# Two layers of a hybrid backbone: the state-space core begun group by group, with the second layer's z columns between the recurrence's

## The chip, the cores and the metric

The kernel runs on one core of one Trainium2 chip. The time is the device time of one execution in microseconds; a version is judged by the median of its runs. An execution's own time is a little longer than its span, which runs from the first to the last instruction in the profile.

## The reference

Two layers work on 256 context tokens and 256 latent tokens of 2048 channels, in float32. In each layer the tokens are normalised and modulated (scale and shift from a conditioning vector), and multiplied by `w_in`. The result's columns feed three groups of heads:

- a gated linear recurrence over time in both directions (columns `lx`, and `lg` for its gate);
- windowed attention with sinks, 8 heads over 2 key heads (`q`, `k`, `v`, and `ag` for its gate);
- a state-space model in both directions, two groups of 8 heads (`x`, `B`, `C`, `dt`, and `z` for its gate).

The state-space part, cut to what matters:

```python
xs, B, C = split(silu(conv(xbc)))            # x: 1024 channels, B and C: two groups of 128
dt = softplus(dt + bias)
for chunk in chunks of 128 tokens:           # forward and backward
    W = (C @ B.T) * decay * dt               # inside the chunk
    y = W @ x + (C @ h) * exp(Acs)           # h: the state that enters the chunk
    h = exp(A_last) * h + B.T @ (x * w_state)
y = rmsnorm(y * silu(z), norm_w)
```

Channels 512g to 512g + 511 of `x` belong to group g, with row block g of `B` and of `C`. The three results, gated, are multiplied by `w_out`, scaled by a gate from the conditioning vector and added to the tokens. The second layer gives latent tokens alone, so its `C`, `z`, `lg`, `q` and `ag` are computed for 256 tokens only, while `B`, `x`, `lx`, `k` and `v` need all 512.

## The kernel before

**Columns.** `w_in` is taken in columns of 128 channels. Each is 16 blocks (128 input channels each) and three matmuls a block (`mm3`): the float32 operands are split into a rounded part `hi` and a remainder `lo`, and hi x hi, hi x lo and lo x hi are summed in one PSUM accumulator (`acc`, three of them). Weights come in tiles `raw` of 8 blocks (512 KB, three buffers); ScalarE makes `hi` (line 237) and VectorE `lo` (line 238). A column is 512 tokens wide, or 256 where layer 2 needs the latent tokens alone. `HEAD` columns (B0, B1, C0, C1, x0, x1, and in layer 1 with `FILL` also x2 to x5) are built side by side over the input channels; `body` lists the others in order, the remaining x first, then lx and lg in pairs, z, k, v, then q and ag in pairs. After that comes the output projection in three parts, for the recurrence, the state-space part and the attention, 16 columns of 8 blocks each.

**Order of work.** TensorE's instructions stand in the order in which the program writes them (`manual_schedule`). What a finished column sets off is a generator (`consume` spawns it), which yields either a time in us or a condition. The planner's clock advances with each matmul by its nominal time (`mm`: 512 columns 0.216 us, four times that for plain float32, less where matmuls run side by side). After each block `pump` steps the tasks whose time has come, and the matmuls they write stand there in TensorE's order. The times are in `WAIT`, one for each layer. `drain(until)` steps the waiting tasks in order of their due times, moves the clock to each, and goes on until its condition holds; no column stands between. The other engines' instructions are ordered by the framework's scheduler, except those given to `keep_in_program_order`: such a one stays behind the instruction that was written before it for its engine.

**State-space core** (`ssd_core`, `State`, `Output`). It waits until 13 tasks have ended (two B, two C, eight x, dt), then goes through group 0 and group 1: 14 steps a group in layer 1, and 10 in layer 2, where the context's outputs aren't needed. A step has a `begin` (VectorE, ScalarE and GpSimd work; an `Output` also loads two tiles `bc` of running sums, broadcast to all partitions) and an `end` (matmuls). Between a step's `begin` and the next lies `WAIT["core"]`; a step's `end` follows one such wait after the next step's `begin`. When all steps have ended, `core_done` is set. `z` columns come behind a drain for `core_done`; `ssd_z` forms z * (1 + tanh(z / 2)) and multiplies `Y` by it. The square sums of `Y` are collected, and at z7 the norm follows.

**Conditioning products** (`ada_wide`). The modulation of layer 2 and both gates are products of a 256 KB row tile `araw` with a broadcast row `adac` on VectorE, summed along the row (line 380); these instructions are kept in program order. Parts 0 to 2 run in layer 1 from the core's end on. Part 3, layer 2's gate, is 64 products in four rows of 16, begun at the end of layer 2's head; after each comes `WAIT["ada1"]`, or `WAIT["ada"]` (5.97 in layer 2) once the core has ended, and it pauses from the core's beginning until its end:

```python
yield self.wait("ada" if self.core_done else "ada1")
if self.ssd_ready == 13 and not self.core_done:
    yield lambda: self.core_done
```

The output projection of layer 2 needs that gate to empty its first accumulator (line 1073), and begins so:

```python
self.drain(lambda: part in self.parts_done)
if pi == 0:
    self.drain(lambda: self.ada_done >= (4 if l else 1))
```

**Attention.** `att_q` writes a head's score matmuls, and then its softmax on VectorE, ScalarE (exp, line 854) and GpSimd (line 864). After `WAIT["q2"]` it writes the transposes (line 870), then the products with v. For head 7 the wait is `WAIT["q2z"]`, 12.98 in layer 2, so that these come after the first blocks of the output projection.

**Buffers.** `SHARED` gives tiles that don't live at the same time one set of buffers: `bc` (four) is shared with `dtw`, `adac`, `kh`; `aw` (three) holds `araw`, `ww` and `part0`; four PSUM tiles `mx` serve all matmuls but the columns'.

## Time and profile before

| | |
|---|---|
| median of 3 runs | 1846.21 us (1844.5 to 1850.26) |
| the profiled execution | 1850.27 us, span 1848.5 us |
| TensorE matmul busy | 1777.5 us, 96% of the span |
| VectorE busy | 1424.8 us, 77% |
| ScalarE busy | 959.7 us, 52% |
| GpSimd busy | 334.9 us, 18% |
| HBM read and written | 310.51 MB and 10.63 MB, 174 GB/s over the span |

Busy is the time in which an engine had an instruction in work; matmuls are pipelined and their ends are modelled, so a busy TensorE isn't TensorE at its best. The granted clock is the share of TensorE's full clock (2.4 GHz) that the throttle gave; the other level is 1.2 GHz, or 0.5. A chain is followed back from the last instruction to what released it. In a list of waits, a wait is put down to whatever came last.

### The profile page before, as it was taken

The numbers are of one execution on the slowest core, as the hardware profiler recorded it, in microseconds if no ns is written. First come the engines' busy times: TensorE is split into PE (matmuls) and PEld (weight loads), VectorE is DVE, ScalarE is ACT, GpSimd is POOL, SyncE is SP. The second block draws the span as 40 slices with busy tenths as digits, with TensorE's granted clock in tenths as the row PEclk, the third lists the DMA queues.
The fourth block names the chain that finished last, engine by engine and source line by source line (L and its number), as shares of the span: only waits on it lengthen the run. The fifth ranks groups of instructions, "written<-read, shape, count | busy, mean of one in ns | idle before, by whom it ended". The sixth has DMA issues, their size and how long they took to land.

```text
span 1848.5 us, 29534 instructions
## 1 busy us (share of the span) xinstructions
PE 1777.5 (96%) x10522; PEld 1456.0 (79%) x10522; DVE 1424.8 (77%) x3053; ACT 959.7 (52%) x1766; POOL 334.9 (18%) x271
## 2 busy tenths in 40 slices
PE   7999999999999999999999999999999999999999
PEld 4777876666778877887878887878666788999999
DVE  4447769899998888989999547776778885788765
ACT  4324577777433354555232335544687763677543
POOL 0000124434210022221000020010243330122000
PEclk9999999999999999999999999999999999999999
DMA  9982433435775645557777443464343564555656
GB/s 377 365 295 69 124 97 106 129 111 157 220 219 175 192 145 174 172 166 245 231 221 221 129 126 107 142 183 150 96 136 109 160 202 152 174 174 165 210 184 183
DMA packets 140261, 323.09 MB, mean 175 GB/s; under 512 B 14000, under 2 KB 39504, under 8 KB 139472
## 3 DMA queue, kind: packets, MB, share of 16 engines
q1 hardware_dynamic: 140112, 321.20, 55.6%
q8 instruction: 82, 1.34, 0.3%
q14 instruction: 67, 0.55, 0.1%
HBM read 310.51 MB, written 10.63 MB: 174 GB/s over the span
## 4 chain that ended last, share of the span: by engine, by line
PE 74%; DVE 12%; ACT 7%; issue 4%; DMA 3%; POOL 1%; SPq 0%; POOLq 0%; DVEq 0%; ACTq 0%
PE acc L174 57%; PE mx L174 12%; DVE lo L238 3%; PE ada L174 3%; PE mx L170 2%; DVE ee L1161 1%; DVE ada L380 1%; ACT lt L712 1%; DVE araw L380 1%; ACT hi L237 1%; DMA bc<-acsD 1%; ACT ww L1163 1%; DMA araw<-in_adaw_dram 1%; DVE lh L730 1%; ACT ee L1160 1%
## 5 line engine op out<-in xcount | busy, mean ns | idle before, releaser
L174 PE MATMUL acc<-u,hi 128*128 128x512 f32 (+1 forms) x4800 | 1284.7, 356 | 10.7 <-ACT hi L237 6.2
L174 PEld LDWEIGHTS acc<-u,hi 128*128 128x128 f32 x4800 | 840.6, 191 | 158.3 <-issue 29.0
L174 PE MATMUL acc<-u,lo 128*128 128x512 f32 (+1 forms) x2400 | 848.8, 354 | 24.8 <-DVE lo L238 24.2
L237 ACT ACTIVATE hi<-raw 128x512 fp32r<-128x512 f32 x640 | 399.3, 629 | 588.4 <-PE acc L174 459.2
L238 DVE TENSOR_TENSOR lo<-raw,hi 128x512 fp32r<-128x512 f32 x640 | 470.1, 737 | 195.7 <-ACT hi L237 186.0
L174 PEld LDWEIGHTS acc<-u,lo 128*128 128x128 f32 x2400 | 458.0, 191 | 98.9 <-DVE lo L238 39.0
L380 DVE SCALAR_TENSOR_TENSOR araw<-araw,adac 128x512 f32<-128x512 f32 x256 | 189.5, 741 | 8.6 <-DMA araw<-in_adaw_dram 5.3
L380 DVE SCALAR_TENSOR_TENSOR ada<-araw,adac 128x512 f32<-128x512 f32 x192 | 143.1, 745 | 11.2 <-DMA araw<-in_adaw_dram 6.6
L174 PE MATMUL mx<-u,hi 128*128 128x512 f32 (+1 forms) x320 | 98.8, 392 | 0.0
L1073 DVE SCALAR_TENSOR_TENSOR X<-acc,mod,X 128x256 f32<-128x256 f32 x144 | 65.0, 478 | 38.2 <-PE acc L174 38.0
L864 POOL TENSOR_SCALAR prob<-prob,qrs 128x512 f32<-128x512 f32 (+1 forms) x48 | 58.3, 1228 | 200.0 <-ACT hi L237 158.0
L427 POOL TENSOR_TENSOR ssq<-ssq,sq 128x512 f32<-128x512 f32 (+1 forms) x26 | 32.7, 1257 | 303.2 <-ACT sq L423 303.2
L1172 POOL TENSOR_TENSOR bc<-bc,CT 128x512 f32<-128x512 f32 x40 | 62.2, 1566 | 88.2 <-ACT bc L1171 49.1
L511 POOL TENSOR_SCALAR X<-xs,prm 128x512 f32<-128x512 f32 (+1 forms) x16 | 15.4, 963 | 344.5 <-DVE xs L489 340.6
L174 PEld LDWEIGHTS mx<-u,hi 128*128 128x128 f32 x320 | 55.9, 188 | 14.1 <-issue 4.0
L720 POOL TENSOR_TENSOR la<-lt 128x512 f32<-128x512 f32 x32 | 39.0, 1221 | 134.5 <-ACT lt L718 117.1
L174 PE MATMUL mx<-u,lo 128*128 128x512 f32 (+1 forms) x160 | 60.7, 379 | 0.0
L1161 DVE SCALAR_TENSOR_TENSOR ee<-bc,nacs,ee 128x128 f32<-128x128 f32 x96 | 44.2, 509 | 18.7 <-DMA bc<-acsD 14.3
L767 POOL TENSOR_TENSOR qw<-qw,cst 128x256 f32<-128x256 f32 x20 | 22.5, 1127 | 195.2 <-DVE rt L766 131.5
L727 POOL TENSOR_TENSOR lt<-lt,ltl 128x512 f32<-128x512 f32 x32 | 47.8, 1515 | 48.4 <-ACT ltl L724 45.5
L712 ACT ACTIVATE lt<-mx,gbh 128x512 f32<-128x512 f32 x64 | 42.4, 674 | 10.0 <-PE mx L174 10.0
L174 PE MATMUL mx<-xc,gw 64*64 64x512 f32 x128 | 39.9, 615 | 4.6 <-DVE H L1128 2.2
(236 smaller groups left out, 1979.0 us busy)
## 6 DMA issues: line engine op xcount, KB each, us to landing
raw<-in_w_in_dram SPq DMA_DIRECT2D x224, 512.0 KB, 3.7
araw<-in_adaw_dram SPq DMA_DIRECT2D x256, 256.0 KB, 3.2
raw<-in_w_out_dram SPq DMA_DIRECT2D x96, 512.0 KB, 3.8
ar<-in_ada_dram SPq DMA_DIRECT2D x84, 256.0 KB, 5.9
bc<-acsD SPq DMA_DIRECT2D x48, 256.0 KB, 4.1
ar<-in_ada_dram SPq DMA_DIRECT2D x22, 512.0 KB, 7.4
adac<-condD SPq DMA_DIRECT2D x28, 256.0 KB, 4.6
gw<-in_gates_dram SPq DMA_DIRECT2D x16, 256.0 KB, 2.9
```

The costliest lines, as they stand in the source:

```text
L170: self.nc.tensor.transpose(out=out, in_=lhsT, identity=rhs)
L174: self.nc.tensor.matmul(out=out, lhsT=lhsT, rhs=rhs, start=start, stop=stop, **kw)
L237: nc.scalar.activation(out=hi, in_=part, func=AF.Copy)
L238: nc.vector.tensor_tensor(out=lo, in0=part, in1=hi.bitcast(F32), op=ALU.subtract)
L380: i = nc.vector.scalar_tensor_tensor(out=o, in0=raw, scalar=1.0, in1=row[c].rearrange("p t x -> p (t x)"), op0=ALU.mult, op1=ALU.mult, acc ...
L712: nc.scalar.activation(out=t, in_=pg[g], func=AF.Tanh, scale=0.5, bias=self.gb[:, 16 * g + 8 * d + m:16 * g + 8 * d + m + 1])
L720: nc.gpsimd.tensor_tensor(out=a2, in0=tr, in1=tr, op=ALU.mult)
L727: nc.gpsimd.tensor_tensor(out=ti, in0=ti, in1=tl[:, d], op=ALU.mult)
L864: nc.gpsimd.tensor_scalar(out=pr[j], in0=pr[j], scalar1=rs[:, j:j + 1], scalar2=1.0, op0=ALU.mult, op1=ALU.mult)
L1073: nc.vector.scalar_tensor_tensor(out=x[:, s], in0=acc[:, s.start - w0:s.stop - w0], scalar=mod[:, 2 * KT + m, c:c + 1], in1=x[:, s], op0=A ...
L1161: nc.vector.scalar_tensor_tensor(out=e[:, j], in0=bcs[1][:, j], scalar=k.nacs[:, r:r + 1], in1=e[:, j], op0=ALU.add, op1=ALU.min)
L1172: nc.gpsimd.tensor_tensor(out=bc, in0=bc, in1=k.CT[:, g, None, tok].to_broadcast([P, 4, P]), op=ALU.mult)
```

## The change

`ssd_ready` was a count and is now a set of what has ended. The core waits, before each group, for that group's own B and C, for dt, and for its own four x columns. `core_begun` is set at the first group, and the conditioning products of layer 2 pause from then on. The wait between two core steps goes from 4 to 5.4 in layer 1, and from 5.2 to 9.2 in layer 2. In layer 2 each z column follows its lx and lg in `body`; z * (1 + tanh(z / 2)) is written to the context half of `Y`, which is idle in layer 2, and `Y` is multiplied once the core has ended. The drain for `core_done` stands ahead of the first z column in layer 1 as before, and ahead of the first k column in layer 2.

```diff
--- before.py
+++ after.py
@@ -73,8 +73,9 @@
     done = HEAD[l] + FILL[l]
     b = [("x", i) for i in range(8) if ("x", i) not in done]
     for m in range(8):
-        b += [("lx", m), ("lg", m)]
-    b += [("z", i) for i in range(8)]
+        b += [("lx", m), ("lg", m)] + [("z", m)] * l
+    if l == 0:
+        b += [("z", i) for i in range(8)]
     b += [("k", 0), ("k", 1), ("v", 0), ("v", 1)]
     for m in range(8):
         b += [("q", m), ("ag", m)]
@@ -131,7 +132,7 @@
 
 HB = 3
 WAIT = {"B": (36.48, 14.89), "C": (28.19, 0.27), "x": (33.09, 10.71), "dt": (16.92, 0.59), "softplus":
-        (19.41, 30.37), "acs": (0.94, 0.68), "core": (4, 5.2), "ada": (2.38, 5.97), "ada1": (1.17, 2.75), "z":
+        (19.41, 30.37), "acs": (0.94, 0.68), "core": (5.4, 9.2), "ada": (2.38, 5.97), "ada1": (1.17, 2.75), "z":
         (4.45, 7.93), "lx": (12.81, 15.41), "lx2": (1.16, 0.85), "k0": (6.3, 7.38), "k1": (1.19, 1.72), "k2": (1.86,
         2.04), "k3": (0.82, 6.16), "v": (7.89, 1.43), "q0": (2.04, 1.29), "q1": (5.86, 3.7), "q2": (7.82, 11.04),
         "q2z": (42.1, 12.98), "q3": (0.5, 1.1), "q4": (2.82, 1.03)}
@@ -382,7 +383,7 @@
                                                            op1=ALU.mult, accum_out=sums[:, c, m, q:q + 1])
                         self.tc.keep_in_program_order(i)
                     yield self.wait("ada" if self.core_done else "ada1")
-                    if self.ssd_ready == 13 and not self.core_done:
+                    if self.core_begun and not self.core_done:
                         yield lambda: self.core_done
             mod = self.mods[l][:, KT * part:KT * part + KT]
             o = PARAMS["ada_b"][0] + KT * part
@@ -512,7 +513,7 @@
                                     op0=ALU.mult, op1=ALU.mult)
             yield self.wait("x")
             self.tok_major(xs, self.Xtok[:, :, i * P:(i + 1) * P])
-        self.ssd_ready += 1
+        self.ssd_ready.add((kind, i))
 
     def dt_weights(self, l):
         nc = self.nc
@@ -586,7 +587,7 @@
         self.acsD = self.dram([P, P], "acsD")
         nc.sync.dma_start(out=self.acsD, in_=at)
         yield self.wait("acs")
-        self.ssd_ready += 1
+        self.ssd_ready.add(("dt", 0))
 
     def softplus(self, z, n, tag):
 
@@ -612,9 +613,11 @@
     def ssd_core(self, l):
 
 
-        yield lambda: self.ssd_ready == 13
         ends = []
         for g in range(2):
+            need = {("B", g), ("C", g), ("dt", 0)} | {("x", 4 * g + i) for i in range(4)}
+            yield lambda: need <= self.ssd_ready
+            self.core_begun = True
             f1, r1 = self.ssd_state(0, g, 0), self.ssd_state(1, g, 1)
             steps = [f1, r1]
             if l == 0:
@@ -645,7 +648,7 @@
     def ssd_z(self, l, i, pz, t0):
         nc = self.nc
         th = self.t([P, 512], "cth")[:, t0:]
-        zz = self.t([P, 512], "cv")[:, t0:]
+        zz = self.Y[:, i, :C] if l else self.t([P, 512], "cv")
         nc.scalar.activation(out=th, in_=pz, func=AF.Tanh, scale=0.5)
         nc.vector.scalar_tensor_tensor(out=zz, in0=th, scalar=1.0, in1=pz, op0=ALU.add, op1=ALU.mult)
         if not self.core_done:
@@ -947,8 +950,8 @@
         nc = self.nc
         self.l = l
         mod = self.mods[l]
-        self.ssd_ready = self.kv_ready = 0
-        self.core_done = False
+        self.ssd_ready, self.kv_ready = set(), 0
+        self.core_begun = self.core_done = False
         self.lru_h, self.att_o, self.parts_done, self.mixes = {}, {}, set(), {}
         t0 = lambda kind: 0 if l == 0 or kind in CTX_COLS else C
         wst = self.blocks(self.a["w_in"][l], NW)
@@ -1035,7 +1038,7 @@
             self.spawn(self.ada_wide((0, 1, 2)))
         for ct in body(l):
             s = t0(ct[0])
-            if ct == ("z", 0):
+            if ct == (("z", 0), ("k", 0))[l]:
                 self.drain(lambda: self.core_done)
             if ct == ("k", 0):
                 self.att_begin(l)
```

## Rows read from the trace of the kernel before

**Rows 1.** The page, part 4: the chain that ended last, by engine.

```profile
PE 74%; DVE 12%; ACT 7%; issue 4%; DMA 3%; POOL 1%; SPq 0%; POOLq 0%; DVEq 0%; ACTq 0%
```

**Rows 2.** Stages: length; PE, PEld, DVE, ACT, POOL busy; clock; DMA share; GB/s.

```profile
218.00:474.00 256.00, 238.83 (x1255) 172.31 (x1252) 219.30 (x395) 184.39 (x356) 97.38 (x69) 0.99 0.43 130
...
1219.00:1271.00 52.00, 49.51 (x217) 39.83 (x216) 36.70 (x71) 21.98 (x43) 9.35 (x8) 0.93 0.59 181
1271.00:1475.00 204.00, 191.36 (x1139) 146.72 (x1138) 159.61 (x264) 147.74 (x255) 67.85 (x54) 0.97 0.41 125
1475.00:1530.00 55.00, 50.08 (x384) 46.57 (x383) 44.68 (x74) 35.18 (x62) 16.00 (x15) 0.97 0.66 203
1530.00:1704.00 174.00, 173.07 (x1235) 161.92 (x1234) 129.06 (x289) 110.76 (x211) 37.45 (x34) 1.00 0.54 164
```

**Rows 3.** Readers of finished columns, layer 2: count, ns min/median/max, first and last start.

```profile
L460 ACT ACTIVATE cv<-acc,scwh x6: 759/762/772, 1208.2 to 1271.9; 128x512 f32<-128x512 f32 x6
...
L649 ACT ACTIVATE cth<-acc x8: 367/370/385, 1481.0 to 1529.4; 128x256 f32<-128x256 f32 x8
...
L895 ACT ACTIVATE agt<-acc x8: 384/385/386, 1592.2 to 1704.5; 128x256 f32<-128x256 f32 x8
```

**Rows 4.** Waits of TensorE, 1219 to 1530: us in total, times, longest.

```profile
PE acc L174 <- DVE lo L238: 9.3, 10, 2.3
...
PE mx L174 <- ACT lt L712: 3.9, 4, 1.4
```

**Rows 5.** VectorE by line, 1284 to 1460: count, busy us, mean ns, idle before.

```profile
L238 DVE TENSOR_TENSOR lo<-raw,hi 128x512 fp32r<-128x512 f32 x56 | 47.8, 857 | 11.6 <-ACT hi L237 9.5 <-PE acc L174 2.0
...
L1164 DVE SCALAR_TENSOR_TENSOR ww<-cbm,dt,ww 128x128 f32<-128x128 f32 x32 | 10.1, 364 | 0.6 <-ACT ww L1163 0.6
...
L1147 DVE TENSOR_TENSOR cbm<-mx,cst 128x128 f32<-128x128 f32 x8 | 1.9, 277 | 0.0
```

**Rows 6.** Line 380 in 1160 to 1231, to 1290, and 1450 to 1704.

```profile
L380 DVE SCALAR_TENSOR_TENSOR araw<-araw,adac x19: 674/684/883, 1163.8 to 1226.2; 128x512 f32<-128x512 f32 x19
...
L380 DVE SCALAR_TENSOR_TENSOR araw<-araw,adac x32: 674/684/1787, 1163.8 to 1275.9; 128x512 f32<-128x512 f32 x32
...
L380 DVE SCALAR_TENSOR_TENSOR araw<-araw,adac x32: 672/684/1782, 1460.2 to 1677.3; 128x512 f32<-128x512 f32 x32
```

**Rows 7.** Timeline of TensorE, ScalarE and GpSimd, 1698 to 1714: start, length, instruction.

```profile
1699.88 0.40 PE L174 MATMUL mx<-kh,ql 128*128 128x512 f32 x1
...
1705.38 0.40 PE L174 MATMUL acc<-u,hi 128*128 128x256 f32 x2
...
1708.13 0.77 ACT L854 ACTIVATE prob<-mx,qng,qsc 128x512 f32<-128x512 f32 x1
...
1710.94 2.56 POOL L864 TENSOR_SCALAR prob<-prob,qrs 128x512 f32<-128x512 f32 x2 [13.87 <-DVE qrs L858]
```

**Rows 8.** The page, part 6: DMA issues, KB each, us from issue to landing.

```profile
araw<-in_adaw_dram SPq DMA_DIRECT2D x256, 256.0 KB, 3.2
...
bc<-acsD SPq DMA_DIRECT2D x48, 256.0 KB, 4.1
```

**Rows 9.** The chain in order of time, its last long piece: start, us, what.

```profile
1722.67 122.06 PE acc L174 x1017
```

**Rows 10.** Busy time in two short stretches, columns as in rows 2.

```profile
1243.00:1247.00 4.00, 1.70 (x6) 0.99 (x7) 3.63 (x6) 4.00 (x8) 1.80 (x2) 0.85 0.11 20
1247.00:1252.00 5.00, 5.00 (x14) 4.04 (x13) 4.93 (x8) 1.35 (x3) 2.53 (x2) 0.50 0.81 242
```

**Rows 11.** Timeline of SyncE's queue and VectorE, three rows of layer 2.

```profile
1276.60 0.33 SPq L1154 DMA_DIRECT2D bc<-acsD  x1
...
1434.36 0.90 SPq L1154 DMA_DIRECT2D bc<-acsD  x2
...
1448.79 0.68 DVE L1167 TENSOR_TENSOR ee<-ee,ww 128x512 f32<-128x512 f32 x1
```

**Rows 12.** Weight splits on VectorE over the whole span, columns as in rows 5.

```profile
L238 DVE TENSOR_TENSOR lo<-raw,hi 128x512 fp32r<-128x512 f32 x640 | 470.1, 737 | 195.7 <-ACT hi L237 186.0 <-PE mx L174 3.6 <-PE acc L174 2.0
```

## The prediction

> **What bounds the kernel now.** The page comes first, and on it the chain that ended last: 74% of the span is TensorE, 12% VectorE [rows 1]. Matmul work is unchanged by this diff, so only time in which TensorE stands still or runs at its lower clock can be won, and only time of the same two kinds can be lost.
>
> The table of stages says where such time is [rows 2]. In each stretch I take its length less PE's busy time, and add (1 - granted clock) x length. Layer 1, 218 to 474 us (x7 read to the last lg): 17.2 + 2.6 = 19.8 us. Layer 2, 1219 to 1271 (x4 to x7): 2.5 + 3.6; 1271 to 1475 (the lx/lg pairs, beside which the state-space core runs): 12.6 + 6.1; 1475 to 1530 (z): 4.9 + 1.6; together 31.5 us of 311. From 1530 to 1704 (k, v, q, ag): 0.9 us of 174. These are the ceilings of the gain: 31.5 and 19.8. The places of the stretches come from the instructions that read a finished column [rows 3]; the x columns stand 12.7 us apart, so x3, second of those six, is read near 1220.
>
> The list of PE's waits in 1219 to 1530 names VectorE's `lo` split as the largest (9.3 us in 10 waits) and further down the recurrence gates' tanh on ScalarE (3.9) [rows 4]: weights arrive late because VectorE is behind. Its queue in the core's stretch holds 56 splits at 857 ns, and eight lines of the core, from 10.1 us down to 1.9, 51 us in all [rows 5]. VectorE's busy time over the time PE needs (length less what was lost) is 159.6 / 185.3 = 86% in the core's stretch, and PE loses 9% there; it is 129.1 / 173.1 = 75% in 1530 to 1704, where PE loses 0.5% [rows 2].
>
> **What the change does, part by part.** *Core spread in layer 2.* It used to begin after x7; now it begins when B0, C0, dt and x0 to x3 are there, four columns earlier. By the planner's arithmetic (a column of 512 adds 48 x 0.216 = 10.4, of 256 5.2) x3's end to z7's end is 248 on the planner's clock: 4 x 10.4 for x4 to x7, 8 x 20.8 for the triples, 40 for gates, core and transposes. Twenty-one core intervals were 5.2 + about 1.4 each (their own matmuls 1.05, rounding to the next look at the tasks 0.35); now 9.2 + 1.4 = 10.6, 223 in all. Begun 12 after x3, the core ends at 235: 13 before z7 ends, so the drain moved to k0 finds nothing left. VectorE's work in 1219 to 1530 is 36.7 + 159.6 + 44.7 = 241 us, less some 23 ada products of 0.68 [rows 6] that move away, 225; PE needs 279.5: 81%, where the core's stretch had 86%. Between the two points above (0.5% lost at 75%, 9% at 86%), 81% gives 5%, some 13 to 14 us lost instead of 31.5. **Gain 18**; bounds 0 and 31.5.
>
> *Kept silu.* Eight 256-wide products go to the idle context half of `Y` instead of `cv`: same count, same size, nothing. When the core ends, seven pending `y` products of 256 columns come at once, about 0.4 us each as an estimate from 0.68 for 512 [rows 6]; columns already supplied hide them, and it is 3 us if that cover is gone.
>
> *Core spread in layer 1.* Begin moves from x7 + 33.1 to x3 + 33.1 on the planner's clock, about 25 earlier. Tasks are looked at every 0.647 in full columns, so 4 rounds up to 4.53 and 5.4 to 5.82, plus 1.0 of own matmuls: 29 intervals take 199 instead of 161, and the core ends about 13 later, 3 before z0's drain. No work moves between engines. VectorE stands at 219.3 / 236.2 = 93% there [rows 2], and falls to about 88% with x6 and x7's time taken in. That is no quiet stage either: **gain 6**, bounds 0 and 19.8. The ada products that wait for this core start 13 later and are all asked for only in the last columns of the layer's projection: nothing, 13 if that cover is gone.
>
> *What becomes late: the ada products of layer 2.* There are 64, pinned in VectorE's order, paused while the core runs. Before: 32 by 1276, before the core, and 32 from 1460 to 1677, 7.0 us apart (217.1 / 31), done 27 us before the last ag column is read [rows 3, 6]. After: the pause begins near 1231, where the trace has 19 [rows 6]. So 45 remain when the core ends, 13 us before z7's end. To the last ag column there are then 174 + 13 = 187 us, room for 27. **Eighteen are left** when `layer` reaches `drain(lambda: self.ada_done >= 4)`. This drain served nothing before.
>
> It serves tasks by due time and sets the clock to it: 18 steps of 5.97 move it by 107. Head 7 of the attention waits there too, due after 12.98 (q2z). So its transposes and products enter PE's order ahead of the output projection; before, 13 planner-us of the projection stood between. In the trace its last score matmul is issued at 1699.88, its exp runs at 1708.13, GpSimd's two scalings end at 1713.5, while PE had gone on at 1705.38 with the projection [rows 7]. Unsheltered, PE transposes at 1712.2 and, after copies, splits and the products, is free near 1716: 1716 - 1705.4, less 2.2 of head 7's own PE work, is 8.4; if ScalarE reaches the exp sooner, 4. Then some 15 ada products, behind head 7's gating in VectorE's order. A row takes 3.2 us to land [rows 8] and 0.68 to multiply; with three buffers and some 0.3 from product to next issue that is 1.4 each, the first three already there: 18 us, so the gate is ready near 1734. The projection's columns take 122.06 / 1017 x 24 = 2.9 us [rows 9] and three accumulators hold until 1716 + 8.7; then PE waits 9. Bounded by VectorE alone (15 x 0.68) it waits 2; behind weight loads, 16. Each of the two stalls can be followed by slow clock: after 2.3 us of idling in 1243 to 1247 the next 5 us were granted 0.50, the level of 1.2 GHz [rows 10], 3.4 us lost with its edges; I take 1 each, bounds 0 and 3.4. **Loss 19** (8.4 + 9 + 2), bounds 6 and 31.
>
> A rule that bears on this: the Trainium skill, "TensorE: Matmul & The Clock Gate", section "Part 2: What happens when you issue a matmul", says that only weight loads are pulled ahead while the matmuls themselves stay in program order. By it head 7's wait holds up the whole projection, as I count it; were matmuls free to pass, the first 8.4 would be nothing and the sum 8 lower. The waits on ACT `lt` in [rows 4], with ready columns behind them, agree with the rule.
>
> *A buffer held.* The old pause fell on a boundary of 16 products, where no `adac` row is live; 19 falls inside one, and `adac` shares four buffers with the core's `bc`. So the core of layer 2 has three, and the second half-group of each pair of outputs loads its last `bc` only when the first is finished, one step earlier. The trace shows such a buffer: the fourth `bc` load goes out at 1276.60, right behind the 32nd product [rows 6, 11]. From load to finished weights took 1434.36 to 1449.47, 15 us [rows 11]; at its shortest it is 4.1 to land [rows 8] and, as an estimate, 5 of arithmetic. A step is about 11.8 us in real time. Four such places: **loss 3**, bounds 0 and 14.
>
> *The sum.* -18 - 6 + 19 + 3 = -2 us against the profiled execution of 1850.3 us (span 1848.5 and 1.8 around it): 1848.3. The median of the three runs is 4.1 lower than that execution, so 1844.
>
> **The rivals.** *A, forecast, 0.40:* gains and the late drain nearly cancel; 1836 to 1852.
>
> *B, 0.20: the late products are mostly hidden.* ScalarE gives the exp early and rows land fast, so the drain costs 8: 1833. For it: DMA share is 0.54 there. Against: PE's order is fixed by the program.
>
> *C, 0.18, slower: the spread buys little.* Every VectorE product stays, and splits stay long: 857 ns in the core's stretch, with GpSimd's work beside them, against 737 over the whole kernel [rows 5, 12], which layer 1 at 93% does not escape. Layer 2 gains 8 and layer 1 2, so the drain decides: +12, 1858. It decides from where both gains are under 16. The Trainium skill, "SBUF — State Buffer", section "Who interferes with whom", gives such a mechanism: a VectorE instruction with two SBUF inputs and a GpSimd one that reads SBUF exclude each other. By it the spread moves these clashes and removes none, which would give C's 1858; 857 against 737 fits it.
>
> *D, 0.12, slower: three `bc` buffers bind.* At 15 us per chain, each of four places waits 3 us and idling drops the clock: +14 instead of +3, 1855. It decides from 2 us a place.
>
> *F, 0.10: the spread takes nearly all of it*, 28 and 14: -20, 1826.
>
> Against no change, 0.3% (5.5 us) is about what a measurement here can tell. Faster: 0.3 of A, 0.9 of B, all of F, 0.40. Slower: 0.2 of A, 0.9 of C, 0.75 of D, 0.33. Same: 0.27. The range leaves out half of F below and the far ends of C and D above: 1827 to 1861.
>
> **What would show it.** Right: PE's idle and half-clock time in the stage x4 to z7 falls below 20 us; 19 products of L380 before the core and some 18 after the last ag column; a PE gap behind head 7's `prob` and one behind `mod` in the first projection columns. Wrong: no such gaps (B), PE waits on `bc` or `ee` at every second output of layer 2 (D), or waits on `lo` unchanged (C).

## The result, and the profile after

The changed kernel takes 1887.79 us (median of 4 runs, 1885.62 to 1892.19), against 1846.27 for the kernel before on the same chip: a ratio of 1.0222, 95% interval 1.02 to 1.0244. That is slower, by 41 us, where 1844 was forecast, and outside the range. The profiled executions are 1885.62 and 1850.27 us, 35 apart.

Where do the 35 us lie? The readers of finished columns tell. Layer 2's first one stands 12 us later than before (1185.3, where it was 1173.3); its last z column 4 later, its last ag column 7 later; the first emptied accumulator of the output projection 39 later, and from the sixth on the distance stays at 35. The first three rows below are the columns x2 to x7 (with one of 256, a C column, ahead of them), z and ag as in [rows 3]; the last one, the accumulators, has its first start at 1747.3, where it was 1708.

```profile
L461 ACT ACTIVATE cv<-acc,scwh x7: 550/763/772, 1192.6 to 1283.3; 128x512 f32<-128x512 f32 x6, 128x256 f32<-128x256 f32 x1
L652 ACT ACTIVATE cth<-acc x8: 359/366/384, 1309.2 to 1533.1; 128x256 f32<-128x256 f32 x8
L898 ACT ACTIVATE agt<-acc x8: 384/385/388, 1599.7 to 1711.8; 128x256 f32<-128x256 f32 x8
L1076 DVE SCALAR_TENSOR_TENSOR X<-acc,mod,X x6: 475/484/484, 1747.3 to 1759.1; 128x256 f32<-128x256 f32 x6
```

The table of stages, cut at such readers (columns as in [rows 2]), first of the kernel before: layer 1 up to z0, layer 2 from x4 to z7, z7 to the last ag.

```profile
184.00:488.00 304.00, 286.83 (x1486) 210.03 (x1485) 259.37 (x474) 213.80 (x403) 106.23 (x78) 0.99 0.43 130
...
1232.00:1529.00 297.00, 276.95 (x1665) 221.80 (x1664) 231.24 (x388) 198.95 (x348) 90.45 (x74) 0.97 0.47 144
1529.00:1705.00 176.00, 175.07 (x1247) 163.70 (x1247) 130.98 (x294) 112.54 (x215) 37.45 (x34) 1.00 0.53 163
```

The same of the changed kernel, with a fourth row for the stretch up to the projection's first emptied accumulator:

```profile
184.00:502.00 318.00, 293.45 (x1480) 215.18 (x1480) 253.66 (x449) 213.30 (x402) 102.33 (x78) 0.95 0.37 118
...
1244.00:1533.00 289.00, 269.36 (x1650) 217.19 (x1649) 211.48 (x344) 191.35 (x336) 81.62 (x68) 0.98 0.41 128
1533.00:1712.00 179.00, 175.15 (x1242) 161.22 (x1241) 136.90 (x299) 118.48 (x223) 43.73 (x40) 1.00 0.55 175
1712.00:1747.00 35.00, 16.56 (x100) 15.37 (x98) 22.18 (x65) 10.41 (x25) 1.37 (x2) 0.65 0.64 211
```

Each stage's lost time is read from these rows: length less PE's busy time, plus half of the busy time at the lower clock (summed from the trace's clock records, since the clock's column is rounded). Layer 1: 18.9 before, 37.1 after. Layer 2, x4 to z7: 29.5 and 24.2. From z7 to the last ag: 0.9 and 3.8. Behind it: nothing, and 23.2 up to 1747, with 3.6 more up to 1880. The two parts move differently. Idle time alone goes from 17.2 to 24.6 in layer 1, and from 20.0 to 19.6 from x4 to z7; the clock's part goes from 1.7 to 12.5, and from 9.5 to 4.6. Stages called "x7 to z0" below start at 184; up to 217 no kernel here idles.

So layer 1 lost where a gain was forecast, layer 2 gained far less and won back no idle time to speak of, and the end cost more. The chain that ended last doesn't show where (76% PE where it was 74% [rows 1]); the list of PE's waits and its timeline name the end. First the waits of TensorE from 1700 to 1750, then its timeline:

```profile
PE acc L175 <- DVE X L1076: 11.7, 1, 11.7
PE mx L171 <- POOL prob L867: 6.6, 1, 6.6
```

```profile
1712.82 0.41 PE L175 MATMUL mx<-ptlh,vl 128*128 128x256 f32 x1
1719.80 1.97 PE L171 MATMUL mx<-cst,prob 128*128 128x128 f32 x8 [6.57 <-POOL prob L867]
...
1735.90 0.28 PE L175 MATMUL acc<-u,lo 128*128 128x256 f32 x1
1747.92 0.77 PE L175 MATMUL acc<-u,hi 128*128 128x256 f32 x2 [11.75 <-DVE X L1076]
```

Head 7's transposes hold PE until GpSimd has scaled its weights, with the projection's blocks behind them; then three full accumulators wait for the gate. VectorE's timeline shows what the gate waited for: late products, each behind its row's landing, then the sum.

```profile
1744.55 0.69 DVE L381 SCALAR_TENSOR_TENSOR araw<-araw,adac 128x512 f32<-128x512 f32 x1 [2.11 <-DMA araw<-in_adaw_dram]
...
1746.83 0.22 DVE L391 TENSOR_REDUCE mod<-adas 128x16 f32<-128x64 f32 x1
1747.08 0.17 DVE L392 TENSOR_TENSOR mod<-mod,prm 128x16 f32<-128x16 f32 x1
1747.29 1.27 DVE L1076 SCALAR_TENSOR_TENSOR X<-acc,mod,X 128x256 f32<-128x256 f32 x3
```

The count of products, against [rows 6]: 19 ahead of the core, 27 from its end to 1707, and 17 from 1715 on (the remaining one starts at 1711.5).

```profile
L381 DVE SCALAR_TENSOR_TENSOR araw<-araw,adac x19: 681/684/884, 1175.2 to 1244.1; 128x512 f32<-128x512 f32 x19
...
L381 DVE SCALAR_TENSOR_TENSOR araw<-araw,adac x27: 659/684/1230, 1516.4 to 1706.7; 128x512 f32<-128x512 f32 x27
...
L381 DVE SCALAR_TENSOR_TENSOR araw<-araw,adac x17: 682/692/694, 1715.4 to 1746.1; 128x512 f32<-128x512 f32 x17
```

### The profile page after: what moved, and what is told of

The parts are those of the page before. It is cut to its first block, busy times and chain, and to the rows that moved or that the text cites. A ratio compares the mean times of both kernels' runs of the same rounds, so it can differ in the third digit from the quotient of the medians.

```text
span 1883.6 us, 29522 instructions
## 1 busy us (share of the span) xinstructions
PE 1785.8 (95%) x10522; PEld 1462.2 (78%) x10522; DVE 1423.1 (76%) x3053; ACT 960.0 (51%) x1764; POOL 327.3 (17%) x271
## 4 chain that ended last, share of the span: by engine, by line
PE 76%; DVE 12%; ACT 4%; issue 4%; DMA 3%; POOL 1%; SPq 0%; DVEq 0%; POOLq 0%; ACTq 0%
PE acc L175 58%; PE mx L175 14%; DVE lo L239 3%; PE ada L175 2%; DMA araw<-in_adaw_dram 2%; PE mx L171 2%; DMA bc<-acsD 1%; DVE araw L381 1%; DVE ada L381 1%; DVE lh L733 1%; POOL prob L867 1%; DVE ee L1164 1%; DVE ww L1167 1%; DVE xc L467 1%; ACT hi L238 0%
## 5 line engine op out<-in xcount | busy, mean ns | idle before, releaser
L239 DVE TENSOR_TENSOR lo<-raw,hi 128x512 fp32r<-128x512 f32 x640 | 475.1, 746 | 204.3 <-ACT hi L238 191.3
L381 DVE SCALAR_TENSOR_TENSOR araw<-araw,adac 128x512 f32<-128x512 f32 x256 | 183.4, 718 | 14.1 <-DMA araw<-in_adaw_dram 8.6
L1076 DVE SCALAR_TENSOR_TENSOR X<-acc,mod,X 128x256 f32<-128x256 f32 x144 | 65.0, 478 | 36.7 <-PE acc L175 36.6
L1175 POOL TENSOR_TENSOR bc<-bc,CT 128x512 f32<-128x512 f32 x40 | 57.5, 1444 | 124.3 <-ACT bc L1174 95.3
L1164 DVE SCALAR_TENSOR_TENSOR ee<-bc,nacs,ee 128x128 f32<-128x128 f32 x96 | 37.9, 446 | 25.5 <-DMA bc<-acsD 22.2
L725 DVE SCALAR_TENSOR_TENSOR lt<-lt,xc 128x512 f32<-128x512 f32 x32 | 23.4, 731 | 27.8 <-ACT lt L715 27.8
```

The costliest lines, as they stand in the source:

```text
L239: nc.vector.tensor_tensor(out=lo, in0=part, in1=hi.bitcast(F32), op=ALU.subtract)
L381: i = nc.vector.scalar_tensor_tensor(out=o, in0=raw, scalar=1.0, in1=row[c].rearrange("p t x -> p (t x)"), op0=ALU.mult, op1=ALU.mult, acc ...
L1076: nc.vector.scalar_tensor_tensor(out=x[:, s], in0=acc[:, s.start - w0:s.stop - w0], scalar=mod[:, 2 * KT + m, c:c + 1], in1=x[:, s], op0=A ...
L1164: nc.vector.scalar_tensor_tensor(out=e[:, j], in0=bcs[1][:, j], scalar=k.nacs[:, r:r + 1], in1=e[:, j], op0=ALU.add, op1=ALU.min)
L1175: nc.gpsimd.tensor_tensor(out=bc, in0=bc, in1=k.CT[:, g, None, tok].to_broadcast([P, 4, P]), op=ALU.mult)
```

## The experiments

Ratios are to the kernel before, on the same chip, with their 95% intervals. The changed kernel has 1.0222. A string, below, is the eight ScalarE and nine VectorE instructions with which one `Output` forms its weights `ww` and `ee`. Lost times (us), as above:

| | ratio | layer 2 begins | x7 to z0 | x4 to z7 | z7 to ag |
|---|---|---|---|---|---|
| before | 1 | 0 | 18.9 | 29.5 | 0.9 |
| changed | 1.0222 (1.0200 to 1.0244) | +12 | 37.1 | 24.2 | 3.8 |
| layer 1 as before | 1.0140 (1.0123 to 1.0157) | +3 | 22.6 | 24.7 | 4.3 |
| layer 1: early begin alone | 1.0189 (1.0174 to 1.0204) | +5 | 28.4 | 28.7 | 4.6 |
| layer 1: wide steps alone | 1.0199 (1.0163 to 1.0234) | +10 | 40.9 | 23.9 | 4.5 |
| gate in time | 1.0100 (1.0076 to 1.0123) | +13 | 33.5 | 25.2 | 5.5 |
| gate in time, layer 1 as before | 1.0037 (1.0024 to 1.0050) | +3 | 20.4 | 22.8 | 5.0 |

The last four columns come from one execution each. Those with layer 1 untouched scatter from 18.9 to 22.6 in it, so 4 us there say little; their idle time alone is 15.9 to 17.2, the rest of the scatter is the clock's. From x4 to z7 the ten executions with the changed order and begin and with steps of 9.2 (these six, and four below) lose 22.8 to 28.7: 19.6 to 23.1 idle, and 1.5 to 8.1 through the clock.

**Layer 1.** Three kernels complete a table of two by two with the changed one.

```diff
-        "core": (5.4, 9.2)
+        "core": (4, 9.2)                 # first and second kernel
             need = {("B", g), ("C", g), ("dt", 0)} | {("x", 4 * g + i) for i in range(4)}
+            if l == 0:                   # first and third: all 13
+                need = {(k, i) for k in "BC" for i in range(2)} | {("dt", 0)} | {("x", i) for i in range(8)}
```

> The changed kernel with layer 1's core as it was: it begins when all 13 tasks have ended, and its steps are 4 apart; layer 2 stays changed. Theory (layer 1's core lost 12 us, from its x columns to layer 2's begin): those 12 come back whole, layer 2's first readers stand within 2 us of the kernel before, and the whole is 12 us under the changed kernel, 1874. Rival (layer 1's lag is a shift of transfers or of the modulation's products that only moves a wait from one layer to the other): the lag at layer 2's begin goes, but less than 6 us of it is left at the end, 1880 or more.

1875.9 us, and layer 2 begins 3 us late where the theory allowed 2: nearly as it said. The ratio falls by 0.8%, so the loss arises in layer 1 and isn't given back.

> The changed kernel with layer 1's steps 4 apart again, but begun group by group. Theory (the wider spacing costs: more columns have an Output's strings on VectorE and ScalarE beside them, so more of their splits come late): the loss goes, 1874, and the half clock in 217 to 492 us falls from 30 us of the time to under 10. Rival (the early begin costs: the core's work falls on the convolutions of x6 and x7 and on the transposes behind them): the loss stays, 1884 to 1888, and half clock stays above 20 us.

1884.1 us, the rival's time, but layer 2 begins 5 us late, not 12: neither holds. The early begin by itself costs something, though less than both edits; the next kernel tries the other one.

> The changed kernel, layer 1's core begun when all 13 tasks have ended, but its steps still 5.4 apart; with the changed kernel, the early begin alone and layer 1 as before it completes a table of two by two. Layer 2's first x columns were 12, 5 and 3 us later than before in those three. Theory (the two edits add up: the early begin some 4 us, the spacing some 5 to 7): 8 us later than before at layer 2's begin, 1880 us in all, and half clock in 217 to 492 us of some 15 us of the time. Rival (only both together hurt, since only then does the core lie beside the convolutions and reach into the last lx columns): 3 to 4 us later, 1875.

1886.1 us and 10 us late, beyond both: the spacing alone costs nearly all, so the two don't add up. Part of that is this kernel's own: its core isn't done at z0, and in the drain there PE waits for `ee`, 8.2 us in two waits (waits of TensorE, 184 to 507):

```profile
PE mx L175 <- DVE ee L1172: 8.2, 2, 7.0
```

**The end of layer 2.** Only the products' interval changes.

```diff
-        "ada": (2.38, 5.97)
+        "ada": (2.38, 3.0)
```

> The changed kernel with layer 2's conditioning products 3.0 apart behind the core in place of 5.97, so that all 64 are done before the last ag column and the last drain finds nothing to do. Theory (the end of layer 2 lost 28 us through that drain: head 7 ahead of the projection, the gate late, half clock behind each): all of it comes back, 1858, no gap behind prob or mod at the projection's begin. Rival (45 products in a shorter time fill VectorE beside the k, v, q and ag columns, where it stood at 136 of 178 us): PE loses 10 us or more from 1534 to 1712, and 1868 or more is left.

1866.5 us, 1.2% of 1846 or some 22 under the changed kernel; no gap behind `prob` or `mod` is left. The time lies between theory and rival, the mechanism is the theory's. From z7 to the last ag column 5.5 us are lost in place of 3.8. The drain is the cause of the end's loss; the denser products cost little.

> Both edits: layer 1 as before, and layer 2's conditioning products 3.0 apart behind the core. What is left of the change is layer 2's core begun early, its z columns between the recurrence's and the steps 9.2 apart. Theory (layer 2's part is worth 4 to 8 us once nothing else is lost): 1838 to 1842, under the kernel before. Rival (layer 2's part is worth nothing by itself, its 8 us at z7 are given back in k and v or come from VectorE's products moved behind): 1845 to 1850.

1856.6 us, ratio 1.0037: neither theory's time. With the same column matmuls from x4 to the last ag, this kernel needs 289 + 183 = 472 us and the kernel before 297 + 176 = 473. So layer 2's part, freed of the drain, is worth nothing: what is won ahead of z7 (half clock; the idle time is 21.1) is spent behind it.

> Layer 1 as before; in layer 2 the products are 4.0 apart behind the core, so that the last drain finds some 5 in place of 18. Theory (the end's loss has two parts: head 7's transposes ahead of the projection, which any drain of more than 13 us of the planner's clock brings, and the gate, which grows with the products left): the gap behind prob stays at 6 to 8 us with half clock behind it, the gap behind the gate goes or is under 2 us, and of the 30 us some 10 to 14 are left: ratio 1.009 to 1.011. Rival (the loss is in proportion to the products left, the head's part only beside it): a quarter is left, 7 us, ratio 1.005 to 1.007.

(This and all kernels from here on have layer 1's core as before, unless said.) Ratio 1.0088 (1.0057 to 1.0118): the theory. With 5 products left the gate is in time, but head 7's gap is whole, 7.6 us (waits of TensorE, 1700 to 1723), and 1704 to 1723 lose 11.4:

```profile
PE mx L171 <- POOL prob L869: 7.6, 1, 7.6
```

**What spreading is worth in layer 2.** Products beside the core, steps as before, a row's end, the z order, the early begin:

```diff
-                    yield self.wait("ada" if self.core_done else "ada1")
-                    if self.core_begun and not self.core_done:
-                        yield lambda: self.core_done
+                    yield self.wait("ada" if self.core_begun else "ada1")
```

> Layer 1 as before; in layer 2 the conditioning products don't pause for the core but go on beside it, 7.6 apart on the planner's clock, to the ag columns. The kernel with both edits (layer 1 as before, products 3.0 apart behind the core) lost 5.0 us in idle PE from z7 to the last ag column, where the kernel before lost 0.9, and took 1.0037 of the time before. Theory (VectorE's added products cost where they are dense, and little where they are spread): 2 to 3 us of those 5 come back, the core's stretch loses at most 1 more, ratio 1.001 to 1.003. Rival (each product in the core's stretch makes a split late): the stretch x4 to z7 loses 3 us or more above that kernel's 22.8, ratio 1.004 or more.

Ratio 1.0051 (1.0035 to 1.0066), 37.2 lost from x4 to z7 and 2.5 behind it: the rival. That is 14 us more than with the pause, for the 30 products of that stretch, against 2.5 us saved; but 12 of the 14 are half clock, which scatters, and the medians stand only 0.14% (2.6 us) apart, with intervals that overlap: the price is nearer 5 us than 14.

```diff
-        "core": (4, 9.2)
+        "core": (4, 5.2)                 # "ada": 4.9
```

> Layer 1 as before; in layer 2 the core begins early and the z columns stay between the recurrence's, but the steps are 5.2 apart again (the products follow 4.9 apart, all done before the last ag column). Theory (the spacing is what brought x4 to z7 from 30.2 us lost to 22.8): 28 to 31 us lost there, ratio 1.006 to 1.008. Rival (what was lost there follows the splits and GpSimd's work wherever the core lies, and the order of the z columns or the early begin brought the gain): 22 to 25 us lost, ratio 1.001 to 1.004.

Ratio 1.0117 (1.0090 to 1.0144) and 43.7 lost, more than either said and 14 more than before the change: early begin and z order without the spacing do harm. Its waits for `ee`, which the kernel before hasn't, were tested next; this diff is in the next three kernels and in the last three.

```diff
-                    if self.core_begun and not self.core_done:
+                    if self.core_begun and not self.core_done and m == KT - 1:
```

> Two edits in two stages, read apart. Layer 2: as in the kernel with 5.2 between the steps, but the conditioning products pause only at the end of a row of 16, so that no row is held and the core has all four bc tiles (products 4.9 apart behind it). There PE lost 43.7 us from x4 to z7, of which 9.8 in five waits for ee and bc. Theory (the held row takes a bc buffer, and with three the second output of a pair waits, the rival D of the prediction, which 9.2 between the steps hides): the waits for ee and bc go, 30 to 36 us are lost there. Rival (the waits for ee come from VectorE being late with the strings, whatever the buffers): they stay, 41 us or more. Layer 1: begun group by group with steps 4.6 apart; 4 gave 28.4 us lost from x7 to z0, 5.4 gave 37.1. If the loss grows with the spacing: 31 to 34. If it depends on how the steps meet the columns' period: under 26 or over 38.

Layer 2: 36.6, just beyond the theory's 36. The waits of TensorE for `ee`, with the held row (1234 to 1544) and without it (1240 to 1543); 1.3 us of waits for `bc` no longer stand among the five largest:

```profile
PE mx L175 <- DVE ee L1172: 8.7, 4, 3.3
```

```profile
PE mx L175 <- DVE ee L1170: 3.3, 1, 3.3
```

Layer 1: 34.3, in order with 28.4 and 37.1; but 29 products lie ahead of z0 in this kernel, 36 in the one with the early begin alone and 6 in the changed one, so the spacing isn't alone.

> Layer 1 as before; in layer 2 the changed kernel's order and steps of 9.2, the conditioning products pausing only at the end of a row (32 done before the core and 32 behind it, 4.9 apart). The same kernel with the pause inside a row and 3.0 between the products took 1.0037 of the time before; it lost 22.8 us from x4 to z7 and 5.0 from there to the last ag column. Theory (fewer products behind the core, and further apart, cost less beside the attention): 2 to 3 lost after z7, 21 to 25 before it, ratio 1.000 to 1.002. Rival (13 more products fall on the core's first outputs): 26 or more before z7, ratio 1.003 or more.

1850.7 us, ratio 0.9997 (0.9984 to 1.0010), with 2.8 lost behind z7: the theory; the 25.9 ahead of z7 lie between theory and rival. Layer 2's part of the change, repaired, brings no gain that can be told from nothing.

```diff
     for m in range(8):
-        b += [("lx", m), ("lg", m)] + [("z", m)] * l
-    if l == 0:
-        b += [("z", i) for i in range(8)]
+        b += [("lx", m), ("lg", m)]
+    b += [("z", i) for i in range(8)]
...
-                yield lambda: self.core_done
+                yield lambda: self.z_begun       # set behind z0's drain
```

> Layer 2 as in the kernel with the pause on a row's end and steps of 9.2, but with the z columns behind all lx and lg columns, as before the change, so that the z order is tried alone. Theory (z columns between the pairs give the recurrence's strings more room: 4 columns' splits lie between two strings in place of 2): without them 28 to 34 us are lost from x4 to z7. Rival (only the spacing counts): 21 to 26. Layer 1: begun group by group, steps 4 apart, but the conditioning products held until z0 as before the change, where the early begin let them start at 429 us, beside the lx columns. If they were what the early begin cost: under 23 us lost from x7 to z0 (28.4 with them, 18.9 before). If the core's early steps cost it: 26 to 30.

Layer 2: 39.4 lost, 13.5 more than with the z columns between: beyond the theory. Layer 1: 22.7, and layer 2 begins 5 us earlier than before. Once the products are held, the early begin costs nothing there that shows above the scatter (15.2 us idle).

```diff
-        w = k.t([P, 4, P], "ww")
-        for j in range(4):
-            ...
+        nc.scalar.activation(out=e, in_=bcs[0], func=AF.Copy, scale=0.0)
         nc.scalar.activation(out=e, in_=e, func=AF.Exp)
-        nc.vector.tensor_tensor(out=e, in0=e, in1=w, op=ALU.mult)
```

> The changed kernel with its products 3.0 apart behind the core, and with each output's string of weights left out in both layers: the eight ScalarE and nine VectorE instructions that form ee and ww are replaced by one that fills ee with zeros, so the output of the state-space part inside a chunk is missing. It measures how much of the lost time is the strings' at all. Theory (the strings held up the splits behind them in the queues): layer 1 loses under 12 us from x7 to z0 in place of 33 to 37, layer 2 under 10 from x4 to z7 in place of 25. Rival (in layer 2 what is lost is the recurrence's own: its gates, its table loads on ScalarE and its scans, one gap to each pair of columns, wherever the core lies): layer 2 still loses 15 us or more, and no spacing of the core could have brought the 18.

This one has layer 1's core as in the changed kernel. Its stages: x7 to z0, and x4 to z7.

```profile
184.00:471.00 287.00, 281.27 (x1482) 208.44 (x1481) 204.82 (x305) 185.10 (x291) 103.61 (x78) 1.00 0.43 130
...
1214.00:1499.00 285.00, 266.09 (x1652) 215.42 (x1651) 189.66 (x276) 176.91 (x281) 81.50 (x68) 0.99 0.44 130
```

Layer 1 loses 5.7 us in place of 33 to 37: all but these come from the strings. Layer 2 still loses 20.5: the rival. Before the change it lost 29.5, so 9 were to be had, nearly all of it half clock: 18.9 us are idle, where it was 20.0. One of the gaps in the 20.5 is seen at 1364, where no string is; the others aren't resolved. Here ScalarE loads a table, takes the recurrence's root (`ltl`) and then `xc`; VectorE, in order, waits 1.28 us for that `xc` with the split `lo` behind it; and the split lasts 1.79 us, while GpSimd multiplies `lt` from 1360.96 to 1363.49. PE waits for it. ScalarE, VectorE, GpSimd and PE of that kernel:

```profile
1358.24 1.28 ACT L727 ACT_TABLE_LOAD   x1
1359.74 1.15 ACT L727 ACTIVATE ltl<-ltl,epss 128x1024 f32<-128x1024 f32 x1 [0.21 <-DVE ltl L724]
1360.79 0.76 ACT L461 ACTIVATE xc<-acc,prm 128x512 f32<-128x512 f32 x1
...
1361.59 0.75 DVE L467 SCALAR_TENSOR_TENSOR xc<-acc,prm,xc 128x508 f32<-128x508 f32 x1 [1.28 <-ACT xc L461]
1362.25 1.79 DVE L239 TENSOR_TENSOR lo<-raw,hi 128x512 fp32r<-128x512 f32 x1
...
1365.74 0.67 DVE L239 TENSOR_TENSOR lo<-raw,hi 128x512 fp32r<-128x512 f32 x1
...
1360.96 2.53 POOL L730 TENSOR_TENSOR lt<-lt,ltl 128x512 f32<-128x512 f32 x2 [1.81 <-ACT ltl L727]
...
1364.10 0.39 PE L175 MATMUL acc<-u,lo 128*128 128x256 f32 x1 [1.20 <-DVE lo L239]
```

The same form of split took 0.67 us at 1365.74, when GpSimd was idle. The Trainium skill, "SBUF — State Buffer", section "Who interferes with whom", has such a lock between a VectorE instruction with two SBUF inputs and a GpSimd one that reads SBUF; 1.79 beside 0.67 agrees.

**A version that is faster.** Three more kernels, with layer 1's products held until z0 and layer 2's pause on a row's end. The first's difference from the changed kernel (the flag `z_begun` is set behind z0's drain):

```diff
-        "core": (5.4, 9.2), "ada": (2.38, 5.97)
+        "core": (4, 9.2), "ada": (2.38, 4.9)   # second: 3.0, 9.2; third: 4, 7.7, "ada" 4.3
...
-                yield lambda: self.core_done
+                yield lambda: self.z_begun
...
-                    if self.core_begun and not self.core_done:
+                    if self.core_begun and not self.core_done and m == KT - 1:
```

> Layer 1: begun group by group, steps 4 apart as before the change, its conditioning products held until z0. Layer 2: the changed order and steps of 9.2, the products paused only on a row's end and 4.9 apart behind the core. Theory (the early begin in layer 1 gains when the products don't move with it, 22.7 us lost from x7 to z0 in place of 28.4, and layer 2 begins 5 us earlier; layer 2's repaired part is worth 0 to 3): 1840 to 1845, ratio 0.995 to 0.998. Rival (those 5 us were that run's own and layer 1's stages only trade among themselves): ratio 0.999 to 1.001, as with layer 1 as before.

1843.8 us (7 runs, 1841.24 to 1845.58), ratio 0.9960 (0.9945 to 0.9976): faster than the kernel before, and so than the changed one, as the theory said. Layer 2 begins 3 us earlier, and x4 to the last ag takes 289 + 179 = 468 us in place of 473. In layer 1 the 24.3 lost up to z0 are no fewer than before; the 3 us come behind z0, where the trace gives no single cause, and it stays open.

> The same with layer 1's steps 3.0 apart. Theory (in layer 1 a string costs the more, the more columns it is spread over; 4.0, 4.6 and 5.4 lost 22.7 with products held, 34.3 and 37.1): 14 to 20 us lost from x7 to z0. Rival (there is a least near 4, closer steps wait for their own buffers and weights): 25 us or more, with PE waits for ee.

Ratio 1.0020 (1.0009 to 1.0031): the rival. Of the spacings tried 4 is best. 31.6 are lost, over half of it in PE's waits for `ee` (184 to 496):

```profile
PE mx L175 <- DVE ee L1171: 16.4, 6, 6.8
```

> The same as the first of these, but layer 2's core begins when all 13 tasks have ended, as before the change, with steps of 7.7 so that it still ends ahead of k0 (products 4.3 apart behind it). Theory (the z columns between the pairs and the spacing do what there is to be had, the early begin only makes the room): 24 to 28 us lost from x4 to z7, 25.9 in the run with the early begin. Rival (the core's first steps are better placed beside x4 to x7 than further steps beside the pairs): 30 or more.

Ratio 1.0030 (1.0015 to 1.0045), 37.1 lost from x4 to z7 against 23.6: the rival. In layer 2 the early begin counts, with the room for wider steps that it makes.

## Why the prediction was wrong, step by step

The forecast was 2 us less and the profiled execution took 35 more. Of these 37, layer 1 makes 18 (a loss of 12 for a gain of 6), layer 2 up to the last ag column 13 (a gain of 5 for 18), and the end 9 (28 for 19); the held buffer, priced at 3, takes 3 away. Of the signs that I named, the products (19, and 17 late ones) and the two gaps came; less than 20 us lost from x4 to z7 didn't.

**Layer 1 (gain 6, bounds 0 and 19.8) had the wrong sign: a loss of 12.** I took a lower mean load on VectorE for less lost time, and shut out a loss without a reason. The load hardly moved: over the time that PE needs it was 259.4 / 285.1 = 91% before and 253.7 / 281.0 = 90% after, where I had 93% and 88% for a slightly shorter stretch. The lost time rose by 18.2 us all the same, 7.4 of it idle and 10.8 half clock (the stage is 14 us longer and layer 2 begins 12 later; the difference isn't resolved). Nor does the load set the loss elsewhere: it is 88% in all four kernels with the early begin and held products, and they lose 20.7 to 24.3 with steps of 4, and 31.6 with steps of 3.0. The lost time is the strings' (5.7 us without them), and a string does its harm where it meets a column's splits. The changed kernel shows one such place, ScalarE and VectorE ahead of the gaps at 336 and 339 us, and PE behind them:

```profile
334.96 0.39 ACT L1166 ACTIVATE ww<-cbm,dt 128x128 f32<-128x128 f32 x1
335.25 1.14 ACT L238 ACTIVATE hi<-raw 128x512 fp32r<-128x512 f32 x2
...
336.89 0.34 DVE L1167 SCALAR_TENSOR_TENSOR ww<-cbm,dt,ww 128x128 f32<-128x128 f32 x1
337.15 0.73 DVE L467 SCALAR_TENSOR_TENSOR xc<-acc,prm,xc 128x510 f32<-128x510 f32 x1
337.81 1.10 DVE L239 TENSOR_TENSOR lo<-raw,hi 128x512 fp32r<-128x512 f32 x1
...
335.92 0.73 PE L175 MATMUL acc<-u,hi 128*128 128x512 f32 x2 [3.86 <-ACT hi L238]
...
338.96 0.80 PE L175 MATMUL acc<-u,lo 128*128 128x512 f32 x1 [2.31 <-DVE lo L239]
```

`hi` comes behind the last `ww` on ScalarE, `lo` behind `ww` and `xc` on VectorE. In the changed kernel the wider steps make the loss: the core ends later, so that its products begin at 485.7 us, 31 later than before (13 was forecast, on the planner's clock), and only 6 of them lie ahead of z0, where 18 did. Why wider steps cost more isn't shown string by string; that they reach into more columns, up to z0's drain when the begin is late, is an argument. With steps of 4, the early begin costs through the products that it lets start 25 us earlier: 28.4 lost with them (20.4 idle), 20.7 to 24.3 with them held (15.2 to 16.4 idle). What it adds with steps of 5.4 can't be told: 37.1 and 33.5 are lost with it, in two executions, and 40.9 without it, of which 8.2 are waits in the drain.

**Layer 2 (gain 18) was mis-sized: 5.3 less lost ahead of z7, 2.9 more behind it.** Nor are the 5.3 idle time: PE idles 19.6 us where it idled 20.0, and 19.6 to 23.1 in the ten executions with all three edits. What fell is half clock, 9.5 to 4.6, which goes from 1.5 to 8.1 in those ten, and the kernel before has only one trace: that the spread gains anything there isn't shown. PE's waits changed places. Those for `hi` and for the gates' tanh, 4.6 and 3.9 us before, all but went; those for `lo`, by which rival C was to be known, grew from 9.3 us [rows 4] (waits of TensorE, 1244 to 1533):

```profile
PE acc L175 <- DVE lo L239: 17.3, 19, 2.6
```

The ceiling was wrong: I took all 31.5 us as the core's, and 20.5 remain with the strings gone. VectorE's share came out as forecast, 211.5 / (289 - 24.2) = 80% for 81%, with 8% lost for 5%; without strings it is 189.7 / (285 - 20.5) = 72%, and 7.2% is lost, where 75% cost 0.5% among the attention's columns. So the share doesn't set the loss. That the order in the queues does, the recurrence's too, is seen at the places shown, and not for all of the time. The three edits hold only together: without the spacing 36.6 are lost, without the z order 39.4, without the early begin (and at 7.7) 37.1, with all three 22.8 to 28.7; the idle time alone is 28.7, 28.3 and 28.6, against 19.6 to 23.1. And z7's reader, 8 us nearer, shows too much: 16 matmuls on `mx` that stood ahead of it now follow. PE's busy time on `mx` alone, x4 to z7, before and after (length, PE, PEld, DVE, ACT, clock, DMA, GB/s):

```profile
1232.00:1529.00 297.00, 51.43 (x368) 24.57 (x368) 10.41 (x24) 25.80 (x40) 0.97 0.47 144
```

```profile
1244.00:1533.00 289.00, 46.27 (x352) 23.11 (x352) 10.53 (x24) 23.48 (x36) 0.98 0.41 128
```

**The end of layer 2 (loss 19) had the right mechanism, and its clock was mis-sized: 28.** 17 products came late for 18; head 7's stall is 6.57 and two small ones of 1.05 for 8.4; the gate 11.75 for 9. The clock, allowed 2, cost 7.3 (4.7 of the 23.2 and 2.6 of the 3.6 above). Stalls and clock make 26.7; the readers show 28 because some 18 of the projection's matmuls, which stood ahead of the last ag reader, now follow the drain. Five products left instead of 17 still leave 11.4, so head 7's part is fixed and comes with any longer drain. PE stood at 1712.82 before head 7's transposes with the projection behind them. That agrees with the rule cited in the prediction (the Trainium skill, "TensorE: Matmul & The Clock Gate", section "Part 2: What happens when you issue a matmul"): only weight loads pass, matmuls don't.

**The held buffer (loss 3): nothing here.** At 9.2 PE has no listed wait for `ee` from 1244 to 1533. The mechanism exists: at 5.2 it cost 10 us in waits, and 3.3 with the buffer free. The spacing hides it, which the price of 3 didn't allow for.

**The kept silu (nothing)** can't be told from z7 to the last ag, where 2.9 us more are lost: 1.1 of it before the norm's `rs`, the rest on the attention's copies.

Of the rivals, A's cancelling gains don't exist. C came nearest, with layer 2 gaining 8 (8 by the readers, 5.3 by the lost time), and put layer 1's sign wrong too. Its reason, splits that stay long beside GpSimd's work, is borne out as a fact: of 108 weight splits from x4 to z7, 24 took over 0.8 us before and 25 after, each with a GpSimd instruction beside it, and those with none took 0.68 on average (counted in the two traces). But these long splits don't set the loss by themselves: without the strings layer 1 had 23 of them, where the changed kernel had 17, and lost 5.7 us.

## What to carry to other kernels

A ceiling of lost time belongs to whatever makes it: leave the suspected work out once and see what remains before pricing a spread. Mean load says little where in-order queues feed the bottleneck; look at what stands just ahead of the instruction that comes late. Read idle time and half clock apart: here the first repeated to within 1.3 us in untouched code (layer 1, seven executions), while the second went from 1.7 to 6.6. And when work is moved, count what starts or ends with it: at the end of layer 2 the products behind the core cost more than anything that the core's move could have won.

## What the runs showed of the hardware

I had not expected how unevenly the lower clock follows idle time. From 1712.2, around head 7's gap, 17.1 us were granted 0.50, and from 1739.5, over most of the gate's gap and beyond it, 13.7; PE was busy for 9.48 and 5.28 of them (columns as in [rows 2]):

```profile
1712.20:1729.30 17.10, 9.48 (x42) 8.50 (x41) 10.17 (x33) 7.05 (x20) 1.37 (x2) 0.50 0.49 162
1729.30:1739.50 10.20, 6.88 (x58) 6.67 (x56) 7.32 (x18) 3.16 (x5) 0.00 (x0) 1.00 0.83 276
1739.50:1753.20 13.70, 5.28 (x25) 5.31 (x26) 6.68 (x19) 0.63 (x1) 0.00 (x0) 0.50 0.40 132
```

In layer 1 of the changed kernel 24.6 us of idling went with 12.5 us of slow clock, in layer 2, x4 to z7, 19.6 with 4.6. Layer 1's waits for weights are long (13.1 us in 6 for `lo`, 7.2 in 3 for `hi`), layer 2's short (17.3 in 19). That short pieces of idle time keep more of the 2.4 GHz isn't shown by this, though: the kernel before, whose waits from x4 to z7 are 2.3 us at most, lost 9.5 us through the clock with 20.0 of idling, and the ten executions named above lost 1.5 to 8.1 with 19.6 to 23.1.
